# Zero products ahead of the first weights, factors spread by TensorE, both token halves in turn in a hand-set order, and the last products by column halves

## The chip, the cores and the metric

The kernel runs on one core of one Trainium2 chip. The metric is the device time of one execution in microseconds; three executions of the kernel before were timed, and one execution was profiled instruction by instruction.

## The reference

Two transformer blocks are applied to 256 tokens of 1024 features, all in fp32: nine sublayers, each with a norm before and after and a residual. Only the first and the last of them are touched by the change. The first sublayer begins with

```python
def rms_norm(x, g):
    y = x * lax.rsqrt(jnp.mean(x * x, axis=-1, keepdims=True) + EPS)
    return y * g

h = rms_norm(x, pre_mix_g)
z = h @ w_in                       # 1024 -> 2560 columns
za, zb, zc = z[..., :512], z[..., 512:2048], z[..., 2048:]
# za: gelu, then a gated spatial unit; zb: attention of 8 heads;
# zc: gated by a sigmoid, then a causal convolution of 31 taps
```

and the last one ends with `h + 0.5 * rms_norm(f, g)`, where `f` is the feed-forward's down projection of 2816 hidden features.

## The kernel before

**Tiling.** The tokens lie in two halves of 128 on the partitions. All weights come from memory as one stream of 452 pieces of 128 x 1024 fp32 in the order of their use (`w_dma`, line 113, issued by SyncE into four `raw` slots). Each piece is split into a hi part (`w_hi`, ScalarE, line 126) and a lo part (`w_lo`, VectorE, line 135), which go to one of eleven `whl` slots; a `raw` slot is free after the lo part. Operands are split in the same way (`hilo`, lines 187 and 188), and each product is three TensorE products: hi by hi, hi by lo, lo by hi (`mm3`, lines 182 to 184, or `piece_pass`, line 376).

**Order.** The program is traced once; a scheduler then sets each engine's order by its own estimate of the times, taking the instructions by the order of the trace where several are ready. Weight splits count as traced 300 instructions later. On the chip every engine takes its instructions in that fixed order.

**Memory.** Slots of SBUF (`sml`, `big`) and the eight banks of PSUM are handed out in turn: the one that was given back first is taken first.

**Start.** `run` loads the first half of `x`, the identity, the first norm's gains (host-made copies for all 128 partitions, two tiles of 128 x 512), three weight pieces, the second half of `x`, further pieces. ScalarE squares both rows of 512 columns (`squares`, line 258), GpSimd makes r in two instructions (`rsqrt2`, lines 217 and 220), VectorE makes h (`pre_vec`, line 246), TensorE transposes it (`feat4`, line 330), and `hilo` makes the feature-major parts. The second half's norm is a generator (`rest`) that `xstage` steps on beneath the first half's products.

**First products.** `xstage` runs eight k-tiles of 1024 columns for the first half of the tokens (48 products of 512 columns), keeping the eight pieces; then, in the mixer, `mid` makes the first gated tile of the convolution's input (`glu(0)`, 48 products of 256 columns) and loads the memory; then the same eight pieces serve the second half. `each` does Gelu, a layer norm and the values of a half. `glu(1)` comes after that; then `bg` holds the convolution's taps, which `pump` traces by three.

**End.** `boundary` ends each sublayer: the last seven k-tiles of the first half by column halves, its norm (`chain`), the last seven of the second half k-tile by k-tile, the two column halves within each. For the last sublayer the generator's tail (lines 277 to 295) is the end of the program.

## Time and profile before

| | us |
|---|---|
| three runs | 1443.32, 1440.42, 1439.56 |
| median | 1440.42 |
| profiled execution: span from first to last instruction | 1443.3 |
| profiled execution: its own time, the first of the three runs | 1443.32 |

The span and the time of that execution agree, so nothing lies outside the span. The rows below are from this one execution; it is the slowest of the three, 0.2% above the median. Times in rows are counted from the span's start. TensorE is PE (PEld its weight loads), VectorE is DVE, ScalarE is ACT, GpSimd is POOL, SyncE is SP.

### The profile page before, as it was taken

What the parts mean: (1) busy time and instruction counts of PE and PEld (TensorE: products, weight loads), DVE (VectorE), ACT (ScalarE), POOL (GpSimd) and SP (SyncE); (2) the same over time, 40 slices, a digit from 0 to 9 for tenths busy, and PEclk for the clock granted to TensorE, in tenths of its full rate; (3) what the DMA queues carried; (4) which work ended last, traced back from release to release, by engine and by line L of the source; (5) the groups of instructions that cost most, each with busy time, mean ns of one, the idle gap of its engine ahead of it and who ended that gap; (6) DMA issues with size and microseconds to landing.
All of it is one profiled execution on the core that took longest, in us unless ns stands there. A gap on an engine that the chain in (4) does not pass through costs nothing.

```text
span 1443.3 us, 22986 instructions
## 1 busy us (share of the span) xinstructions
PE 1406.3 (97%) x9052; PEld 1271.7 (88%) x9052; DVE 924.2 (64%) x1283; ACT 749.7 (52%) x1226; POOL 141.7 (10%) x160
## 2 busy tenths in 40 slices
PE   7999999999999999999899999999999998999998
PEld 5887998999989999889779999899998887899997
DVE  5998857655566555679776555665556798665552
ACT  6775645544455445466564444554445665554441
POOL 1132001000010000136410000100001132100000
PEclk9999999999999999999999999999999999999999
DMA  8735644655547555453256555475555543365540
GB/s 272 267 106 203 206 146 166 221 191 191 186 154 241 185 197 202 161 175 118 103 198 211 190 187 182 153 239 189 196 193 176 203 153 124 132 219 189 179 159 30
DMA packets 77276, 259.49 MB, mean 180 GB/s; under 512 B 8816, under 2 KB 10224, under 8 KB 77168
## 3 DMA queue, kind: packets, MB, share of 16 engines
q1 hardware_dynamic: 77168, 258.02, 52.1%
q8 instruction: 71, 1.16, 0.3%
q14 instruction: 37, 0.30, 0.1%
HBM read 256.94 MB, written 1.05 MB: 179 GB/s over the span
## 4 chain that ended last, share of the span: by engine, by line
PE 54%; issue 32%; DVE 6%; POOL 3%; ACT 2%; DMA 2%; SPq 0%; POOLq 0%; DVEq 0%; ACTq 0%
PE bank L182 15%; PE bank L183 15%; PE bank L184 15%; PE bank L376 6%; DVE whl L135 2%; DMA raw<-in_w 2%; PE bank L330 1%; ACT whl L126 1%; POOL st L217 1%; PE bank L660 1%; POOL st L220 1%; PE bank L903 1%; DVE sml L607 1%; PE bank L617 0%; DVE sml L651 0%
## 5 line engine op out<-in xcount | busy, mean ns | idle before, releaser
L135 DVE TENSOR_TENSOR whl<-raw,whl 128x1024 fp32r<-128x1024 f32 x448 | 550.8, 1236 | 284.1 <-ACT whl L126 281.3
L126 ACT ACTIVATE whl<-raw 128x1024 fp32r<-128x1024 f32 x452 | 474.1, 1056 | 327.3 <-PE bank L184 164.1
L182 PE MATMUL bank<-big,whl 128*128 128x256 f32 x1824 | 519.9, 285 | 0.0
L184 PE MATMUL bank<-big,whl 128*128 128x256 f32 x1824 | 517.5, 284 | 0.2 <-DVE whl L135 0.2
L183 PE MATMUL bank<-big,whl 128*128 128x256 f32 x1824 | 517.7, 284 | 0.0
L182 PEld LDWEIGHTS bank<-big,whl 128*128 128x128 f32 x1824 | 351.1, 192 | 4.4 <-issue 0.2
L183 PEld LDWEIGHTS bank<-big,whl 128*128 128x128 f32 x1824 | 351.0, 192 | 3.2
L184 PEld LDWEIGHTS bank<-big,whl 128*128 128x128 f32 x1824 | 350.9, 192 | 0.4 <-DVE whl L135 0.4
L182 PE MATMUL bank<-whl,big 128*128 128x512 f32 x640 | 253.1, 396 | 0.0
L183 PE MATMUL bank<-whl,big 128*128 128x512 f32 x640 | 250.7, 392 | 0.0
L184 PE MATMUL bank<-whl,big 128*128 128x512 f32 x640 | 249.3, 391 | 0.0
L376 PE MATMUL bank<-whl,big 128*128 128x512 f32 x768 | 181.1, 394 | 2.5 <-ACT big L187 2.5
L376 PEld LDWEIGHTS bank<-whl,big 128*128 128x128 f32 x768 | 144.6, 190 | 33.1 <-ACT big L187 3.2
L184 PEld LDWEIGHTS bank<-whl,big 128*128 128x128 f32 x640 | 120.4, 188 | 25.9
L182 PEld LDWEIGHTS bank<-whl,big 128*128 128x128 f32 x640 | 120.9, 189 | 22.3
L183 PEld LDWEIGHTS bank<-whl,big 128*128 128x128 f32 x640 | 120.9, 189 | 21.0
L217 POOL TENSOR_SCALAR st<-st 128x1 f32<-128x1 f32 x38 | 18.4, 485 | 917.9 <-ACT sml L277 839.5
L520 ACT ACTIVATE sml<-bank 128x256 f32<-128x256 f32 x72 | 27.7, 384 | 129.4 <-PE bank L184 129.4
L521 DVE TENSOR_TENSOR sml<-sml,bank 128x256 f32<-128x256 f32 x72 | 30.4, 422 | 71.3 <-ACT sml L520 71.3
L187 ACT ACTIVATE big<-bank 128x512 fp32r<-128x512 f32 (+2 forms) x81 | 43.9, 565 | 36.8 <-PE bank L330 30.9
L188 DVE TENSOR_TENSOR big<-bank,big 128x512 fp32r<-128x512 f32 (+2 forms) x81 | 51.1, 652 | 15.4 <-ACT big L187 15.0
L280 DVE SCALAR_TENSOR_TENSOR sml<-bank,sml 128x512 f32<-128x512 f32 x36 | 24.1, 687 | 51.1 <-ACT sml L277 51.0
(161 smaller groups left out, 1018.8 us busy)
## 6 DMA issues: line engine op xcount, KB each, us to landing
raw<-in_w SPq DMA_DIRECT2D x452, 512.0 KB, 3.3
sml<-in_gains SPq DMA_DIRECT2D x38, 256.0 KB, 3.7
sml<-in_na_bias SPq DMA_DIRECT2D x16, 256.0 KB, 3.1
sml<-in_alibi SPq DMA_DIRECT2D x8, 192.0 KB, 4.1
x<-in_x SPq DMA_DIRECT2D x4, 256.0 KB, 5.5
big<-in_mem SPq DMA_DIRECT2D x1, 1024.0 KB, 5.8
out_x<-x SPq DMA_DIRECT2D x4, 256.0 KB, 2.1
sml<-in_gate_ln SPq DMA_DIRECT2D x1, 256.0 KB, 6.1
```

Of the source, the lines that this page charges most:

```text
L126: self.nc.scalar.activation(out=t[:, 0], in_=raw, func=AF.Copy)
L135: eng.tensor_sub(out=t[:, 1], in0=raw, in1=t[:, 0].bitcast(F32))
L182: mm(out, lhsT=ah, rhs=bh, start=first, stop=False)
L183: mm(out, lhsT=ah, rhs=bl, start=False, stop=False)
L184: mm(out, lhsT=al, rhs=bh, start=False, stop=last)
L187: self.nc.scalar.activation(out=hi, in_=src, func=AF.Copy)
L188: self.nc.vector.tensor_sub(out=lo, in0=src, in1=hi.bitcast(F32))
L217: self.nc.gpsimd.tensor_scalar(out=t, in0=a, scalar1=b, scalar2=EPS, op0=ALU.add, op1=ALU.add)
L280: nc.vector.scalar_tensor_tensor(out=t, in0=acc[j], scalar=factor, in1=self.post_g[j], op0=ALU.mult, op1=ALU.mult)
L376: self.nc.tensor.matmul(acc[j], lhsT=x, rhs=p[:, part, c], start=first, stop=last)
L520: nc.scalar.activation(out=t[:, 0], in_=outs[0], func=AF.Silu)
L521: nc.vector.tensor_tensor(out=t[:, 0], in0=t[:, 0], in1=outs[1], op=ALU.mult)
```

## The change

- `run`: the gain tiles of 128 x 512 are no longer loaded at the start; two rows of 1 x 512 (`grow`) are. A tile of zeros (`warm`, 128 x 512) and a row of ones are filled by VectorE. One weight piece instead of three is asked for before the second half of `x`. The first half's norm is not made in `run`.
- The mixer calls `xstage_both` instead of `xstage`. In it the order of TensorE, ScalarE and VectorE is the written one up to the second k-tile: 10 products of zeros into a bank that is never read; two products of the ones by the gain rows, which put the factors on all partitions in two banks; 8 products of zeros; the first half's norm and transposes, each followed by 2 products of zeros; the weight splits between; the second half's norm; both halves' products with the first two k-tiles. From the third k-tile on the two halves take turns with each piece, in the scheduler's order. `glu(0)` and the memory's load come after all of it.
- `squares2`: one row of 512 columns by ScalarE, the other by VectorE.
- `last_half`: the last sublayer's second half takes all seven k-tiles for the first 512 columns, then for the others; the first columns' square, its EPS and its product with the gains are traced between. GpSimd adds the two mean squares and takes the power; the two stores go out on SyncE's and on ScalarE's queue.

Comments and docstrings are gone too; `hilo` and `feat4` return an instruction that nobody uses.

```diff
+    def squares2(self, half):
+        ss = self.st(2)
+        junk = [self.S.get([128, 512]) for _ in range(2)]
+        x = [self.x[:, half, 512 * j : 512 * j + 512] for j in range(2)]
+        self.nc.scalar.activation(
+            out=junk[0], in_=x[0], func=AF.Square, scale=1.0 / 32, accum_out=ss[:, 0:1]
+        )
+        self.nc.vector.tensor_tensor_reduce(
+            out=junk[1], in0=x[1], in1=x[1], scale=1.0 / 1024, scalar=0.0,
+            op0=ALU.mult, op1=ALU.add, accum_out=ss[:, 1:2],
+        )
...
+    def xstage_both(self, ft, specs, each, early=None):
+        nc = self.nc
+        junk = self.B.get([128, 512])
+        gb = [self.B.get([128, 512]) for _ in range(2)]
+        acc = [[self.B.get([128, 512]) for _ in range(2)]]
+        ps = {}
+        def idle(n):
+            for _ in range(n):
+                nc.tensor.matmul(junk, lhsT=self.warm[:, 0:128], rhs=self.warm, start=True, stop=True)
+        def split():
+            self.w_hi()
+            self.w_lo()
+        def products(half, k):
+            if k not in ps:
+                ps[k] = self.W(specs[k])
+            xh, xl = self.kt(ft, k, half)
+            self.piece_pass(acc[half], xh, ps[k], 0, k == 0, False)
+            self.piece_pass(acc[half], xh, ps[k], 1, False, False)
+            self.piece_pass(acc[half], xl, ps[k], 0, False, k == KT - 1)
+        engines = {mybir.EngineType.PE, mybir.EngineType.Activation, mybir.EngineType.DVE}
+        with self.tc.manual_schedule(engines=engines):
+            idle(10)
+            for j in range(2):
+                nc.tensor.matmul(gb[j], lhsT=self.ones, rhs=self.grow[j], start=True, stop=True)
+            idle(8)
+            h0 = self.pre_vec(0, self.squares2(0), gb)
+            split()
+            for j in range(2):
+                self.feat4(0, h0[j], ft[j])
+                idle(2)
+            split()
+            ss = self.squares2(1)
+            h1 = self.pre_vec(1, ss, gb)
+            split()
+            products(0, 0)
+            products(0, 1)
+            for j in range(2):
+                self.feat4(1, h1[j], ft[j])
+            split()
+            self.S.put(*h0, *h1, *self.start_tiles)
+            self.B.put(junk, *gb)
+            acc.append([self.B.get([128, 512]) for _ in range(2)])
+            for k in range(2):
+                products(1, k)
+                self.done(ps.pop(k))
+        for k in range(2, KT):
+            for half in range(2):
+                products(half, k)
+                if k == KT - 1:
+                    each(half, acc[half])
+            self.done(ps.pop(k))
+            if k == 4 and early is not None:
+                early()
...
+        if self.pre_g is None:
+            self.last_half(acc[1], lag1, ch, factor)
+            return dst
...
+    def last_half(self, acc, lag, ch, factor):
...
+        for j in range(2):
+            c = slice(512 * j, 512 * j + 512)
+            for n, (first, lhs, get, _) in enumerate(lag):
+                xh, xl = lhs(1)
+                p = get()
+                self.mm3(acc[j], xh, xl, p[:, 0, c], p[:, 1, c], first, n == len(lag) - 1)
+                if not j and n in (1, 3, 5):
+                    next(ch, None)
...
+            nc.scalar.activation(
+                out=junk, in_=acc[j], func=AF.Square, scale=1.0 / 32, accum_out=ss[:, j : j + 1]
+            )
+            if not j:
+                nc.vector.tensor_scalar(
+                    out=ss[:, 2:3], in0=ss[:, 0:1], scalar1=EPS, scalar2=None, op0=ALU.add
+                )
+            nc.vector.scalar_tensor_tensor(
+                out=yg[j], in0=acc[j], scalar=factor, in1=self.post_g[j], op0=ALU.mult, op1=ALU.mult
+            )
...
+        nc.gpsimd.tensor_tensor(out=r, in0=ss[:, 1:2], in1=ss[:, 2:3], op=ALU.add)
+        nc.gpsimd.tensor_tensor(out=r, in0=r, in1=self.mhalf[:, :1], op=ALU.pow)
+        for j in range(2):
...
+            nc.vector.scalar_tensor_tensor(out=xs, in0=yg[j], scalar=r, in1=xs, op0=ALU.mult, op1=ALU.add)
+            q = nc.scalar if j else nc.sync
+            q.dma_start(out=self.out[128:256, c], in_=xs)
...
-        self.xstage(ft, [(("w_in", 0, k, 0, 512), ("w_in", 0, k, 1536, 512)) for k in range(KT)], each, mid, early)
+        self.xstage_both(ft, [(("w_in", 0, k, 0, 512), ("w_in", 0, k, 1536, 512)) for k in range(KT)], each, early)
+        mid()
...
+        grow = [self.S.get([1, 512]) for _ in range(2)]
+        ones = self.S.get([1, 128])
+        nc.vector.memset(ones, 1.0)
+        warm = self.S.get([128, 512], F32R)
+        nc.vector.memset(warm.bitcast(F32), 0.0)
         load_x(0)
+        for j in range(2):
+            row = GAIN_ROWS.index(GAINS[self.phases[0]][0])
+            nc.sync.dma_start(out=grow[j], in_=self.aps["gains"][row, 0:1, 512 * j : 512 * j + 512])
         nc.sync.dma_start(out=self.ident, in_=self.aps["ident"])
-        g = self.load_gain(GAINS[self.phases[0]][0])
-        self.w_dma(3)
+        self.w_dma(1)
         load_x(1)
         self.w_dma()
...
-        h0 = self.pre_vec(0, self.squares(0), g)
-        self.pump()
-        self.to_feat(0, h0, ft)
-        def rest():
...
```

## Rows read from the trace of the kernel before

**Rows 1.** The page, its first line and its part 1 (busy us, share of the span, instructions), the whole execution.

```profile
span 1443.3 us, 22986 instructions
...
PE 1406.3 (97%) x9052; PEld 1271.7 (88%) x9052; DVE 924.2 (64%) x1283; ACT 749.7 (52%) x1226; POOL 141.7 (10%) x160
```

**Rows 2.** The list of waits of TensorE over the whole execution: instruction and line <- what ended the wait: us in total, times, longest us.

```profile
PE bank L330 <- DVE sml L246: 10.9, 4, 7.9
...
PE bank L617 <- DVE sml L607: 6.7, 6, 2.2
...
PE bank L376 <- ACT big L187: 2.5, 1, 2.5
```

**Rows 3.** The timeline of the first 35 us: start us, duration us, engine, line, operation, out<-in, count [idle before <- what ended it]. SPq is SyncE issuing DMAs.

```profile
0.72 0.86 SPq L1504 DMA_DIRECT2D x<-in_x  x2
...
0.80 0.07 DVE L100 MEMSET mhalf<- 128x16 f32 x1 [0.80 <-PEq L1633]
...
5.64 0.57 POOL L220 TENSOR_TENSOR st<-st,mhalf 128x1 f32<-128x1 f32 x1
...
7.06 1.44 DVE L246 SCALAR_TENSOR_TENSOR sml<-x,st,sml 128x512 f32<-128x512 f32 x2 [6.19 <-DMA sml<-in_gains]
...
7.86 1.97 PE L330 MATMUL bank<-ident,sml 128*128 128x128 f32 x8 [7.86 <-DVE sml L246]
...
9.46 1.06 ACT L126 ACTIVATE whl<-raw 128x1024 fp32r<-128x1024 f32 x1 [4.31 <-DMA raw<-in_w]
...
10.73 1.06 ACT L126 ACTIVATE whl<-raw 128x1024 fp32r<-128x1024 f32 x1 [0.21 <-DMA raw<-in_w]
...
11.69 1.07 ACT L187 ACTIVATE big<-bank 128x512 fp32r<-128x512 f32 x2
...
12.32 6.94 PE L376 MATMUL bank<-whl,big 128*128 128x512 f32 x20 [2.50 <-ACT big L187]
```

**Rows 4.** The instructions of tile `x` issued from 1.1 us to 1.6 us (the loads of the first two rows of 512 columns): us from issue to landing.

```profile
DMA to landing us min/median/max: 2.9/3.0/3.1
```

**Rows 5.** Timelines of TensorE in windows of 0.2 us (a row merges the products that the window holds; its first number is the start of the first of them).

```profile
13.34 1.05 PE L376 MATMUL bank<-whl,big 128*128 128x512 f32 x2
...
13.77 1.05 PE L376 MATMUL bank<-whl,big 128*128 128x512 f32 x2
...
17.04 0.62 PE L376 MATMUL bank<-whl,big 128*128 128x512 f32 x2
...
17.26 0.63 PE L376 MATMUL bank<-whl,big 128*128 128x512 f32 x2
```

**Rows 6.** Four stretches (us from the span's start): length, then busy us and instructions of TensorE, its weight loads, VectorE, ScalarE, GpSimd; the granted clock; the share of the DMA engines; GB/s.

```profile
12.32:43.55 31.23, 31.03 (x152) 26.25 (x153) 24.91 (x32) 20.16 (x26) 2.99 (x5) 1.00 0.81 272
...
43.55:58.10 14.55, 14.55 (x121) 14.34 (x119) 13.64 (x27) 12.89 (x18) 0.98 (x2) 1.00 0.83 298
...
58.10:61.40 3.30, 2.09 (x11) 1.50 (x11) 3.08 (x9) 1.88 (x2) 0.00 (x0) 0.97 0.85 305
...
61.40:64.80 3.40, 3.40 (x18) 3.40 (x18) 3.22 (x10) 2.88 (x7) 0.00 (x0) 0.52 0.24 87
```

**Rows 7.** The timeline of the end, columns as in rows 3.

```profile
1436.77 0.39 PE L184 MATMUL bank<-whl,big 128*128 128x512 f32 x1
...
1437.20 0.60 ACT L277 ACTIVATE sml<-bank 128x512 f32<-128x512 f32 x1
...
1437.98 0.30 POOL L217 TENSOR_SCALAR st<-st 128x1 f32<-128x1 f32 x1 [8.57 <-DVE sml L280]
...
1438.37 0.56 POOL L220 TENSOR_TENSOR st<-st,mhalf 128x1 f32<-128x1 f32 x1
...
1439.74 0.99 SPq L295 DMA_DIRECT2D out_x<-x  x2
```

**Rows 8.** VectorE's groups of instructions by line and shape in the first 44 us: out<-in, shapes, count | busy us, mean ns | idle before.

```profile
L135 DVE TENSOR_TENSOR whl<-raw,whl 128x1024 fp32r<-128x1024 f32 x15 | 18.1, 1221 | 5.2 <-ACT whl L126 5.2
...
L1225 DVE SCALAR_TENSOR_TENSOR sml<-sml,dw,sml 128x256 f32<-128x256 f32 x6 | 2.9, 481 | 0.1
...
L246 DVE SCALAR_TENSOR_TENSOR sml<-x,st,sml 128x512 f32<-128x512 f32 x4 | 2.9, 750 | 7.0 <-DMA sml<-in_gains 6.2 <-POOL st L220 0.9
...
L188 DVE TENSOR_TENSOR big<-bank,big 128x512 fp32r<-128x512 f32 x4 | 2.7, 686 | 0.5 <-ACT big L187 0.5
```

**Rows 9.** The same view of VectorE over the whole execution: the smaller sums (here a sum and a running minimum) that one instruction makes with its product.

```profile
L1339 DVE CUSTOM_DVE_ANT_0 sml<-bank,sml 128x256 f32<-128x256 f32 x8 | 3.4, 419 | 0.0
```

**Rows 10.** ScalarE's groups in the first 62 us: the loads of function tables ahead of Gelu and Sigmoid.

```profile
L1174 ACT ACT_TABLE_LOAD x2 | 2.6, 1283 | 0.0
...
L1245 ACT ACT_TABLE_LOAD x2 | 2.6, 1283 | 0.0
```

**Rows 11.** The timeline of TensorE in the first mixer: plain fp32 products of 64 columns.

```profile
91.04 0.78 PE L1370 MATMUL bank<-sml,sml 128*128 128x64 f32 x6
```

**Rows 12.** The timeline of 54 to 67 us, around the first scores.

```profile
54.64 1.99 ACT L126 ACTIVATE whl<-raw 128x1024 fp32r<-128x1024 f32 x2
...
58.26 0.49 DVE L1225 SCALAR_TENSOR_TENSOR sml<-sml,dw,sml 128x256 f32<-128x256 f32 x1
...
59.25 0.38 PE L659 MATMUL bank<-sml,sml 128*128 128x256 f32 x1 [1.14 <-DVE sml L647]
```

**Rows 13.** The timeline of TensorE, a later wait of the same mixer.

```profile
128.63 0.33 PE L342 MATMUL bank<-ident,big 128*128 128x128 f32 x1 [1.69 <-DVE big L1381]
```

More of the change, by code (lines that the diff above doesn't have):

```diff
@@ L186, in hilo @@
     def hilo(self, hi, lo, src):
-        self.nc.scalar.activation(out=hi, in_=src, func=AF.Copy)
+        made = self.nc.scalar.activation(out=hi, in_=src, func=AF.Copy)
         self.nc.vector.tensor_sub(out=lo, in0=src, in1=hi.bitcast(F32))
+        return made
     def table(self, func):
@@ L262, in squares @@
         self.S.put(junk)
+        return ss
+    def squares2(self, half):
[9 more added lines that the diff above has]
+        )
+        self.S.put(*junk)
         return ss
@@ L332, in feat4 @@
         sl = slice(128 * half, 128 * half + 128)
-        self.hilo(dst[:, 0, k0 : k0 + n, sl], dst[:, 1, k0 : k0 + n, sl], s)
+        made = self.hilo(dst[:, 0, k0 : k0 + n, sl], dst[:, 1, k0 : k0 + n, sl], s)
         self.B.put(b)
+        return made
     def feat_both(self, src, dst, n, k0):
@@ L439, in boundary @@
         return dst
+    def last_half(self, acc, lag, ch, factor):
+        nc = self.nc
+        ss, r = self.st(4), self.st()
+        yg = [self.S.get([128, 512]) for _ in range(2)]
+        for j in range(2):
[6 more added lines that the diff above has]
+                    next(ch, None)
+            junk = self.S.get([128, 512])
+            nc.scalar.activation(
[8 more added lines that the diff above has]
+            )
+            self.S.put(junk)
+        for _, _, get, after in lag:
+            self.WHL.put(get())
+            if after is not None:
+                after()
+        nc.gpsimd.tensor_tensor(out=r, in0=ss[:, 1:2], in1=ss[:, 2:3], op=ALU.add)
+        nc.gpsimd.tensor_tensor(out=r, in0=r, in1=self.mhalf[:, :1], op=ALU.pow)
+        for j in range(2):
+            c = slice(512 * j, 512 * j + 512)
+            xs = self.x[:, 1, c]
+            nc.vector.scalar_tensor_tensor(out=xs, in0=yg[j], scalar=r, in1=xs, op0=ALU.mult, op1=ALU.add)
+            q = nc.scalar if j else nc.sync
+            q.dma_start(out=self.out[128:256, c], in_=xs)
+        self.S.put(*yg, *self.post_g)
+        self.B.put(*acc)
     def later(self, spec):
@@ L1506, in load_x @@
                 )
+        grow = [self.S.get([1, 512]) for _ in range(2)]
[3 more added lines that the diff above has]
+        nc.vector.memset(warm.bitcast(F32), 0.0)
         load_x(0)
+        for j in range(2):
+            row = GAIN_ROWS.index(GAINS[self.phases[0]][0])
+            nc.sync.dma_start(out=grow[j], in_=self.aps["gains"][row, 0:1, 512 * j : 512 * j + 512])
         nc.sync.dma_start(out=self.ident, in_=self.aps["ident"])
-        g = self.load_gain(GAINS[self.phases[0]][0])
-        self.w_dma(3)
+        self.w_dma(1)
         load_x(1)
         self.w_dma()
+        self.warm, self.start_tiles = warm, (warm, ones, *grow)
+        self.ones, self.grow = ones, grow
         ft = self.new_feat()
-        h0 = self.pre_vec(0, self.squares(0), g)
-        self.pump()
-        self.to_feat(0, h0, ft)
-        def rest():
-            h1 = self.pre_vec(1, self.squares(1), g)
-            self.S.put(*g)
-            yield
-            for j in range(2):
-                self.feat4(1, h1[j], ft[j])
-                self.S.put(h1[j])
-                yield
-        self.pend = rest()
         self.mt = None
```

## The prediction, made before the change was run

> **What bounds the kernel now.** I read the page first, then who waited for whom on TensorE, then the timeline of the first 65 us and of the last 10, because the diff touches only these two stretches. The reader should see on the page that TensorE is busy 97% of a 1443.3 us span, 37 us short of it [rows 1]. The list of waits says where those 37 us are: 7.9 us before the first transposes, 2.5 us before the first weight product, and else short ones far from the diff, such as six that make 6.7 us [rows 2]; the last 6 us are the end of the last norm. So in the middle TensorE sets the time, and the change can win only what TensorE loses at the two ends.
>
> At the start the chain is: x lands, ScalarE squares it, GpSimd makes r (ready at 6.2), VectorE waits for the gain rows until 7.06, TensorE transposes, then waits for ScalarE, which splits two weight pieces before it comes to the transposes' copy at 11.69; the first weight product starts at 12.32 [rows 3]. These products start 0.43 us apart at 13.8 and 0.22 to 0.23 apart from 17.04 on [rows 5]: 512 columns in 0.43 us is the 1.2 GHz level, in 0.23 the 2.4 GHz one (the view prints a granted clock of 1.00 there, from before its first record). From 12.32 to 43.55, when the second gated tile's products begin, TensorE is busy 31.03 of 31.23 us [rows 6]. 43.55 is the mark against which I sum: by then both kernels must have done 96 wide products, the second half's 8 transposes and the 48 narrow products of the first gated tile.
>
> At the end, the last product starts at 1436.77, and squares, GpSimd's two steps, the residual and the store follow one behind the other to 1443.3 [rows 7].
>
> **The change, part by part, start.** *Zeros and factors.* TensorE can begin when VectorE has filled the zero tile. A 128x16 fill takes 0.07 us [rows 3], any 128x512 instruction of two inputs 0.75 at most [rows 8]; I take 0.5, so 1.5 us. Ten products at 0.43 end at 5.8. Then come the two products that spread the factors, plain fp32, 512 columns. The nearest rows: 0.23 us for 512 columns of the other kind [rows 5], or 8 times that of fp32 products of 64 columns, six of which take 0.78, 0.10 to 0.13 each: 0.8 to 1.0 [rows 11], both at 2.4 GHz, twice that at 1.2. They are of the second kind, so I take 0.88 each. The clock rose 4.7 us after the stream of products began [rows 3, 5]; here that would be 6.2, so the first is done near 6.8, the second at 7.6, and eight more zero products end at 9.4 (8.1 with the cheap price).
>
> *The norm of the first half.* The squares are shared out: the second half row lands at 1.15 + 3.1 = 4.3 [rows 3, 4], and VectorE's squared sum of 512 columns costs about 0.7 (0.42 for 256 [rows 9]). r is ready at 6.05 where it was 6.2. The 6.2 us wait for the gain rows goes, but what is late next is the spread factor itself: h is made from 6.9 to 8.5, where it was 7.06 to 8.50. The factor change alone is worth nothing. It does take 0.5 MB out of the queue: the first weight piece has 1.1 MB up to and with it instead of 1.6 MB, so it should land near 7.7 instead of 9.45. The second piece has the same 2.06 MB as before and lands at 10.7 as before [rows 3].
>
> *First products.* Transposes 9.4 to 9.95, copy 10.0 to 10.6 (0.60), two zero products, the other transposes, copy to 11.6; the first weight product starts at 11.25 instead of 12.32, and at the high level: 1.1 us and 2.3 us won (11 products at 0.43 instead of 0.23 [rows 5]).
>
> *What the hand-set order queues.* VectorE and ScalarE now work in written order. Behind the copy stands the second piece's hi part (1.06, to 12.65), behind that VectorE's lo part (1.22 [rows 8], to 13.9), only then the second half's squared sum (14.6), GpSimd (0.95 for its two steps [rows 7], 15.7) and h (twice 0.75, to 17.2), the third piece's lo part (18.4), the lo part of the second half's first tile (0.69 [rows 8], 19.1). TensorE has only 12 products for this time. It does eight to 13.1, waits for the lo part until 13.95, ends at 14.9, waits for h until 16.5, transposes until 17.7 and does one product. The next one writes the bank that the first transposes of the second half used (banks are handed out in turn: 0 to 4 go to the zeros, the factors and the first half's sums, the four sets of transposes get 5, 6, 7 and 5, so the second half's sums get 6 and 7), so it waits for VectorE's reading of it, 19.15. Before, the same norm ended beneath 48 products and cost TensorE nothing. From there 11 + 72 products at 0.227 and 48 of 256 columns at 0.12 (121 in 14.55 us [rows 6]) take TensorE to 43.75. Against 43.55: +0.2. Without a wait 11.25 and 28.45 of work would make 39.7; the waits of 0.85, 1.6 and 1.4 and some small ones give it back.
>
> The other bound: the cheap factor price, so that only the second piece's landing (10.7) holds the chain: all of it 0.85 earlier, 42.9, which is -0.65. I take the middle, -0.2.
>
> *Elsewhere in the mixer.* Both halves' Gelu now stand together, before the gated products: of the two loads at each of these two lines one may go (1.28 us each on ScalarE [rows 10]). ScalarE is not what TensorE waits for there, so I count 0; the cover is TensorE's 14.55 busy us of 14.55 [rows 6]. The taps of the convolution that VectorE did before 44 us (six in 2.9 us [rows 8]) must come later, in exchange for weight pieces split earlier: 0, if VectorE has room (a rival below). The small loads and the memory's load go out some us later on SyncE's queue behind the weight pieces; they are used from 60 us on, or in the layer norm at 38.
>
> **End.** The same 42 products by column halves. The first columns' square leaves the tail, but it was no part of it: the second square began at 1437.20, after the last product at 1436.77, and the one before it was over by then [rows 7]. The multiply by gains ran beside GpSimd. GpSimd now adds two tensors instead of adding scalars (0.30): 0.30 to 0.56, the price of its power on the same shape [rows 7]; I take 0.4, +0.1. Two stores on two queues instead of one: the second waited for its half of the residual, not for the first store, so 0. A store from ScalarE's queue is not in the trace; SyncE's loads and stores took 0.43 and 0.50 each [rows 3, 7], so 0 with 0.1 either way.
>
> **Sum.** -0.2 + 0.1 = -0.1. The profiled execution's span, 1443.3, is that of the slowest of the three runs, 1443.32; against the median of 1440.42 the sum gives 1440.3 us. What a measurement of this kernel can tell from no change is about 0.3%, 4.3 us: from 1436.1 to 1444.7.
>
> **Rivals.**
> *The waits I worked out don't come, and one behind goes too (faster).* If the second half's norm comes in time (the order of squares and lo parts takes less than I count), TensorE reaches the mark at 40.1 (39.7 and 0.4 of small waits): 3.4 less. After that the first scores wait 1.14 us for VectorE, which is behind a tap and for ScalarE, which is behind two hi parts; the clock is then 0.52 for 3.4 us, worth 1.7 [rows 6, 12]. The work around them is scheduled anew and ScalarE has fewer table loads; without them it is 2.8 less. Together -6.2: 1434.2. For it: those waits rest on nine durations in a row, and a queue that runs an instruction sooner shortens all. Against: each of them is a measured row, and none is counted with a gap.
>
> *The clock falls inside the stage.* From 14.9 to 19.15 TensorE would have about 1.2 us of work. Such a stretch cost the clock at 58: 1.14 idle with light work behind it, then 0.52; 1.69 idle at 128.6 did not [rows 6, 12, 13]. A fall costs 1.7: 1442.0. The Trainium skill, "TensorE: Matmul & The Clock Gate", Part 4, says that transposes don't count as work for the clock as products do; by that the stretch is nearly empty, and this case would be the likely one. The trace here agrees only loosely: the eight transposes at 7.86 [rows 3] did not keep the products at 12.32 from the low level, but 2.5 us of waiting lay between.
>
> *VectorE gets behind (slower).* From 43.55 to 61.4 VectorE is busy 16.7 of 17.85 us [rows 6]. If these taps and the gated product move behind 44 us (2.9 + 0.4, say 3.4 us, with no weight pieces done ahead for it), scores and probabilities wait behind them in its queue: 3.4 and a fall of the clock behind it, 1.7: +5.1, 1445.5. It decides from the point where the pieces split by 44 us are no more than the 15 of before [rows 8].
>
> *The zeros do not raise the clock.* Then 1.2 GHz lasts until the real products have run: factors done at 9.3, zeros at 12.7, first product near 16.1, second half's h at 20.7, the mark near 48: +4.5, 1444.9. Against: nothing but that no row here shows products of zeros.
>
> **Chances.** As summed 0.42; clock falls in the stage 0.20; faster rival 0.22; VectorE behind 0.11; zeros without effect 0.05. The first two are within 0.3%: same 0.62, faster 0.22, slower 0.16. The likeliest is 1440.3. The range runs from just below the faster rival, 1433, to the zeros' case, 1445; a third of the faster case and the VectorE case are left out (0.18).
>
> **What would show it.** Right: the first wide product with weights near 11.3 and 0.23 us apart; waits of TensorE for VectorE's h near 15 to 17 and for a bank near 18; the first products of the second gated tile within a us of 43.5; the last product to the end of span still 6.5 us. Wrong: no such waits, or a mark near 40; a longer gap before the first scores; a granted clock of 0.5 between 18 and 23.

## The result: 12.5 us slower, and the profile after

The changed kernel takes 1454.35 us (median of 4 runs, 1453.95 to 1456.41); the kernel before, run beside it, takes 1441.87 (4 runs, the three above and one of 1443.36). The ratio is 1.0087, 95% interval 1.0069 to 1.0106. The prediction was 1440.3, no change, and none of its rivals reached beyond 1445.5. One run of e2, of 2773.8 us, is left out of its figures below.

One thing about the numbers first. In the runs whose span is on record, those of the kernel before too, the time lies 1.73 to 1.86 us above the span (2.07 to 2.16 in e8). I had taken the span of 1443.3 [rows 1] for the whole time of that execution; by this its time was about 1445.1, and it is none of the three timed runs. It lies 3 us above the median of the kernel before, so the 8.9 us between the two profiles' spans understate the difference of the medians by some 3 us.

The page of the changed kernel, first line and part 1:

```profile
span 1452.2 us, 23043 instructions
...
PE 1420.9 (98%) x9078; PEld 1282.8 (88%) x9078; DVE 922.8 (64%) x1290; ACT 747.0 (51%) x1220; POOL 142.6 (10%) x160
```

TensorE is busy 14.6 us longer than before [rows 1], with 26 more products recorded (the zeros and the factors), and it is short of the span by 31 us instead of 37. That does not mean that it waits less where it matters: 9.8 of the 14.6 us lie ahead of the first weight product, where it stood idle before. From that product to the end (columns as in [rows 6]), first in the kernel before, then in the changed one:

```profile
12.32:1443.33 1431.01, 1404.38 (x9044) 1270.10 (x9044) 921.00 (x1279) 744.35 (x1218) 140.34 (x152) 0.99 0.52 179
```

```profile
13.41:1452.16 1438.75, 1409.07 (x9045) 1274.63 (x9043) 918.08 (x1281) 743.11 (x1215) 141.34 (x152) 0.99 0.54 177
```

There the changed kernel is 7.7 us longer: busy 4.7 longer, for the same products (9044 and 9045 records), and idle 3.0 longer. A product at the lower clock counts as busy for longer (products of zeros start 0.22 us apart at 8.6 and 0.42 apart at 9.6).

The timeline of the start, changed kernel (start us, duration us, engine, line, operation, out<-in, count, [idle before <- what ended it]):

```profile
1.60 4.61 PE L433 MATMUL bank<-sml 128*128 128x512 f32 x10 [1.60 <-DVE sml L1633]
...
6.14 1.98 PE L451 MATMUL bank<-sml,sml 1*128 1x512 f32 x4
...
7.37 1.54 DVE L247 SCALAR_TENSOR_TENSOR sml<-x,st,bank 128x512 f32<-128x512 f32 x2 [2.43 <-issue]
...
8.05 2.58 PE L433 MATMUL bank<-sml 128*128 128x512 f32 x8
...
10.43 1.06 PE L346 MATMUL bank<-ident,sml 128*128 128x128 f32 x4
...
11.67 0.38 SPq L1121 DMA_DIRECT2D big<-in_mem  x1
...
13.41 2.06 PE L393 MATMUL bank<-whl,big 128*128 128x512 f32 x8
...
16.36 1.33 POOL L1392 TENSOR_TENSOR sml<-sml,sml 128x512 f32<-128x512 f32 x1 [3.07 <-DMA sml<-in_tri]
...
17.79 0.30 POOL L218 TENSOR_SCALAR st<-st 128x1 f32<-128x1 f32 x1
...
19.59 1.89 PE L346 MATMUL bank<-ident,sml 128*128 128x128 f32 x8 [1.93 <-DVE sml L247]
```

The zeros run from 1.60, the factor products from 6.14 to 8.05, and the first weight product starts at 13.41 (12.32 before [rows 3]). SyncE sends for the memory at 11.67. GpSimd multiplies the mask at 16.36, ahead of the second half's r at 17.79, and TensorE waits 1.93 us for that half.

Stretches of the changed kernel, columns as in [rows 6]; the granted clock is the third number from the end:

```profile
6.09:9.50 3.41, 3.41 (x11) 1.90 (x11) 2.09 (x3) 1.06 (x1) 0.09 (x1) 1.00 1.01 334
9.50:12.91 3.41, 3.41 (x14) 2.73 (x12) 1.23 (x2) 0.60 (x1) 0.00 (x0) 0.50 1.03 386
...
46.64:64.10 17.46, 14.56 (x122) 14.35 (x120) 16.04 (x28) 13.10 (x18) 0.57 (x1) 1.00 0.77 251
64.10:70.90 6.80, 6.55 (x25) 5.65 (x26) 5.30 (x15) 3.94 (x8) 0.00 (x0) 0.50 0.19 69
91.40:94.80 3.40, 3.40 (x17) 3.40 (x18) 2.44 (x8) 0.91 (x2) 0.00 (x0) 0.50 0.02 5
```

The clock is up at 6.09 and down again from 9.5 to 12.9. It falls once more behind the wait of 1.93, at 19.7 for 3.4 us. From 64.1 it is down for 6.8 us, where before it was down for 3.4 [rows 6], and at 91.4 for 3.4, where before it was up.

The mark, the start of the second gated tile, is at 46.64 instead of 43.55. From there to the first scores (the first products of queries and keys with each other, in the attention) TensorE has the same 14.55 us of work as before [rows 6]. What stands ahead of these scores, changed kernel:

```profile
58.90 1.04 ACT L126 ACTIVATE whl<-raw 128x1024 fp32r<-128x1024 f32 x1
60.34 1.06 ACT L126 ACTIVATE whl<-raw 128x1024 fp32r<-128x1024 f32 x1 [0.40 <-DMA raw<-in_w]
61.31 0.36 ACT L762 ACTIVATE sml<-bank 64x256 fp32r<-64x256 f32 x1
...
59.02 2.46 DVE L1345 SCALAR_TENSOR_TENSOR sml<-sml,dw,sml 128x256 f32<-128x256 f32 x6
61.40 1.22 DVE L135 TENSOR_TENSOR whl<-raw,whl 128x1024 fp32r<-128x1024 f32 x1
...
64.35 0.58 PE L779 MATMUL bank<-sml,sml 128*128 128x256 f32 x1 [3.15 <-DVE sml L767]
```

The products of the first queries and keys end near 58.3 (the mark and two gated-size tiles of 5.8). ScalarE makes their hi and lo parts only at 61.31, behind two weight pieces, one of which it waits for; VectorE does six taps and a split meanwhile. TensorE waits 3.15 us, where it waited 1.14 [rows 12].

So the 8.9 us between the profiles arise thus: 3.1 up to the mark, 2.0 from it to the first scores, 2.9 from there to the first norm's squares (at 136.27 before, 144.29 after), and 0.9 in the other 1300 us.

The end, changed kernel:

```profile
1445.68 0.39 PE L184 MATMUL bank<-whl,big 128*128 128x512 f32 x1
...
1446.87 0.19 POOL L550 TENSOR_TENSOR st<-st 128x1 f32<-128x1 f32 x1 [8.55 <-ACT sml L535]
...
1449.18 0.38 ACTq L557 DMA_DIRECT2D out_x<-x  x1
```

From the last product to the end of the span it is 6.5 us, as before (6.6).

### The profile page after: what moved, and what is told of

The parts are those of the page before. It is cut to its first block, busy times and chain, and to the rows that moved or that the text cites. A ratio compares the mean times of both kernels' runs of the same rounds, so it can differ in the third digit from the quotient of the medians.

```text
span 1452.2 us, 23043 instructions
## 1 busy us (share of the span) xinstructions
PE 1420.9 (98%) x9078; PEld 1282.8 (88%) x9078; DVE 922.8 (64%) x1290; ACT 747.0 (51%) x1220; POOL 142.6 (10%) x160
## 4 chain that ended last, share of the span: by engine, by line
PE 55%; issue 31%; DVE 6%; POOL 3%; DMA 2%; ACT 2%; POOLq 0%; DVEq 0%; ACTq 0%; SPq 0%
PE bank L182 15%; PE bank L183 15%; PE bank L184 15%; PE bank L393 5%; DMA raw<-in_w 2%; DVE whl L135 2%; ACT whl L126 1%; PE bank L346 1%; PE bank L780 1%; POOL st L221 1%; POOL st L218 1%; PE bank L779 1%; DVE sml L727 1%; PE bank L737 0%; PE bank L1023 0%
```

## The experiments

"Before" is the kernel before, run beside each; times are medians. Letters name theories of what loses the time, as their texts use them: A, the start and the mixer behind it; B, the second store queue costs time outside the span; C, the gated products come late; D, chance in the scheduler's order; E, the mask multiply ahead of r; S, the order of both halves in turn; L, loads issued early; V, VectorE's sum of work; O, the order of work on VectorE.

**The end.**

```
e1: before, with the changed end (last_half)
e2: changed, with both last stores on nc.sync
```

> The kernel before with the last sublayer's end by column halves alone (its two stores on SyncE's and ScalarE's queues). The start is that of before. Theory A (the whole loss comes from the start and the mixer behind it): the end inside the span is shorter by 0.1, so the time is that of before, 1441.9 within 1. Theory B (a store on a second queue costs about 1.75 us outside the span, since the changed kernel's times are 1.75 above its spans and those of before equal theirs): 1.6 more, 1443.5, with the span unchanged.

> The changed kernel with both last stores on SyncE's queue. Theory B: the time falls by 1.75 to about 1452.6, and time and span agree again. Theory A: 1454.3, with time and span still 1.75 apart.

e1: 1442.38 against 1442.61, ratio 1.000 (0.9987 to 1.0014). e2: 1452.07, ratio 1.0074 (1.0046 to 1.0101). The end is worth nothing that shows within 2 us, and B is dead: time and span differ by the same 1.8 us with one queue and with two. Both are of further use below: in their profiles every engine of e1 has the order of the kernel before up to the last norm, and every engine of e2 that of the changed kernel, so they are second executions of the same order.

**The gated tile early; GpSimd in written order too.**

```
e3: changed, with mid() and its pieces behind the fifth k-tile
e4: changed, with   engines = {PE, Activation, DVE, + Pool}
```

> The changed kernel with the first gated tile's products (and their two weight pieces, and the memory's load) after the fifth k-tile instead of after the eighth. Theory C (VectorE is behind at the first scores, because the convolution's taps can only start after the gated tile): taps run before 44 us again, the wait before the first scores falls from 3.15 to 1 or less, the fall of the clock there from 6.8 us to 3.4 or none: 4 to 5 less, 1449.5. Theory D (the loss after 46 us is chance of the scheduler's order, whatever VectorE does): no less than 2 us gained. The loss of 3.1 us up to the mark stays in both.

> The changed kernel with GpSimd among the engines whose order is the written one. In the changed kernel GpSimd multiplies the spatial weights by their mask (1.33 us, after its load) ahead of the second half's r. Theory E (that multiply makes the second half's h late): r comes 1.2 us earlier, h at 17.5 instead of 18.78, the wait of TensorE before the second half's transposes falls from 1.93 to about 0.7, the mark (end of the first gated tile) from 46.6 to 45.4, the time to 1453.1. The rival: TensorE waits for the lo part of the second piece and the bank anyway, and the mark moves by less than 0.5.

e3: 1455.46, ratio 1.0096 (1.0075 to 1.0117); nothing won, and the wait for the first scores grew to 4.6 us. That leaves C open rather than dead: one tap ran before 44 us (six in the kernel before), and 12 stood ahead of the first scores, as many as in the changed kernel. e4: 1451.26, ratio 1.0069 (1.0043 to 1.0095). The edit missed its aim: the mask multiply still ran ahead of r, since the written order holds inside its block alone. So e4 is, engine by engine and from start to end, a third execution of the changed order. Its profile is of its shortest run, 1445.9, while the three others took 1449.8 to 1452.9: the same program, 4 to 7 us apart, and one execution only 3.3 us over before. In the profiled one the clock doesn't fall between 25.3 and 649.9 us, and the wait for the first scores is 0.82 us; ScalarE and TensorE there:

```profile
58.61 1.06 ACT L126 ACTIVATE whl<-raw 128x1024 fp32r<-128x1024 f32 x1 [0.26 <-DMA raw<-in_w]
59.58 0.36 ACT L763 ACTIVATE sml<-bank 64x256 fp32r<-64x256 f32 x1
...
62.76 0.38 PE L780 MATMUL bank<-sml,sml 128*128 128x256 f32 x1 [0.82 <-DVE sml L768]
```

The mark is 0.7 us later than in the changed kernel's profile, but the piece ahead of the parts is split at 58.61 instead of 60.34, the parts begin at 59.58 instead of 61.31, and the first scores at 62.76 instead of 64.35. In e2 the three times are 61.63, 62.59 and 65.81, the wait 3.44. One order, three executions: the scores come 3.0 to 3.2 us after the parts begin, and the parts come right behind that piece.

**The parts alone.**

```
e5:  before + a tile of zeros; 18 products of it ahead of the first transposes, 6 behind each four
e6:  changed start, but then   self.xstage(ft, ..., each, mid, early)   as before
e12: before's start and end, with xstage_both (no zeros, gains as tiles)
```

> The kernel before with one thing added: VectorE fills a tile of zeros, TensorE makes 18 products of it before the first transposes and 6 after each of the two groups of four. What the warm clock alone is worth: before, the 11 products from 12.32 to 16.9 ran 0.43 us apart instead of 0.23, which is 2.3 us. If the clock that the zeros raise holds through the start, the mark (start of the second gated tile's products, 43.55 before) comes at 41.2 and the time is 2 to 2.5 us under before's, provided that nothing behind takes it back. If it falls between the zeros and the first products, as it did in the changed kernel at 9.5 us, the mark stays within 1 us of 43.55 and the time within 1 us. If VectorE alone sets the mixer's time (theory V below), the mark is earlier but the first norm's end (136.3 before) is not.

> The changed kernel with its start (zeros, spread factors, shared squares, written order up to the first half's transposes) but with the old order behind it: first half, first gated tile, second half, with the second half's norm beneath the first half's products. Theory S (the order of both halves in turn loses the time: the second half's norm in the open, and the first gated tile late, so that the convolution's taps come late): first product near 13.4 as in the changed kernel, no wait for the second half's h, mark between 42 and 44, the wait for the first scores back to about 1 us, time within 3 us of before's. If instead the start itself does the harm (the factors' products and the fall of the clock behind them), the mark stays near 46 and the time 8 to 12 us over before's.

> The kernel before (its start without zeros, its squares on ScalarE, its gains as tiles, its end) with only the stage changed: both halves in turn in the written order, the gated products behind. Theory S (the order loses it): 7 to 10 us over before's time; the mark 2 to 4 us late, for the second half's norm in the open; the wait for the first scores 3 us or more instead of 1.14, since both halves' Gelu, gate norms and gated products fall between the mark and the scores, and a longer fall of the clock behind it. If the loss needs the new start together with the order, this kernel is within 3 us of before's.

| kernel | time | before | ratio (95%) |
|---|---|---|---|
| e5 | 1443.58 | 1441.91 | 1.0009 (0.9992 to 1.0025) |
| e6 | 1446.27 | 1441.91 | 1.0025 (1.0011 to 1.0039) |
| e12 | 1450.34 | 1443.93 | 1.0045 (1.0027 to 1.0062) |

The start loses 4.4 us and the order 6.4, each give or take 2, in all 10.8 of the 12.5. e12's mark is at 42.17, earlier than in before's profile and level with e1's 42.04: the second half's norm in the open costs next to nothing there, against what S expected. What follows the mark does it, here the timeline of e12's first scores, and then its stretches:

```profile
60.73 0.58 PE L764 MATMUL bank<-sml,sml 128*128 128x256 f32 x1 [4.00 <-DVE sml L752]
```

```profile
42.17:60.50 18.33, 14.56 (x122) 14.35 (x120) 17.28 (x31) 12.47 (x19) 2.95 (x3) 1.00 0.83 302
60.50:67.30 6.80, 6.58 (x25) 5.68 (x26) 5.79 (x16) 2.54 (x3) 0.00 (x0) 0.50 0.72 244
```

VectorE is busy 17.28 of 18.33 us, TensorE waits 4.00, and the clock is down for 6.8 us (and again from 81.0). e5 is the contrast; its stretches:

```profile
11.25:55.96 44.71, 43.75 (x273) 38.95 (x273) 39.57 (x60) 34.23 (x44) 3.98 (x7) 1.00 0.86 303
55.96:100.00 44.04, 43.34 (x284) 37.06 (x285) 41.66 (x97) 35.37 (x86) 15.92 (x13) 1.00 0.44 143
```

Its first product comes at 11.25, its mark at 41.19, and the clock stays up from 4.7 to 643 us. Yet its median is no better than before's. In this profile 2.2 of the 4.8 us that it is ahead at 150 us are lost by the last product, and other runs of before are as fast as it.

**What stands ahead of the first scores.**

```
e7:  changed, gains loaded as tiles of 128 rows, idle(18) for idle(10), two factor products, idle(8)
e8:  changed, SIDE_TAPS = 10 (one more tile slot)
e9:  changed, one column of lng, wst, tri and the memory written from h1 before they are loaded
e10: changed, the taps released behind qk_parts(0), which writes a column of their sum (one more slot)
e11: e7 and e10 together
```

> The changed kernel with the norm's factors loaded as two tiles of 128 rows, as before, instead of one row that TensorE spreads; 18 products of zeros follow one another. Everything behind is as changed. Theory: the two factor products (0.9 us each, light work for TensorE) are what the clock fell behind, at 9.5 us in the changed kernel, and what put the first product at 13.41. In the kernel with zeros alone, without them, the clock rose at 4.7, did not fall again, and the first product came at 11.25. Then here: no fall at 8 to 10, first product 11.2 to 11.7, mark about 44.5 instead of 46.6, time 2 to 4 us lower than the changed kernel's. If the fall belongs to the pauses between zeros, transposes and products, it comes here too, and the time stays within 1 us.

> The changed kernel with ten of the convolution's taps on ScalarE and GpSimd instead of six (and one more tile slot, without which they don't fit). It takes 8 instructions of 0.48 us from VectorE, 3.9 us, between the mark and the end of the mixer, and gives ScalarE 8 of 0.5. Theory V (VectorE, which idles only 1.5 of 17.7 us before the first scores, sets the mixer's time): the time falls by 3 to 6 us, the wait of 3.15 us for the first scores shrinks. If TensorE with its falls of the clock sets it (theory S or L), the mark does not move and the time falls by less than 2 us.

> The changed kernel with the small loads of the mixer and the load of the memory held back: each of four tiles gets one column written by VectorE from the second half's h, so that its load cannot start before about 20 us. In the changed kernel SyncE issued them at 5.7 to 11.7 us, ahead of weight pieces, 1.8 MB that take 4.6 us at 0.4 MB per us; before, it issued them at 23 to 37. Theory L (the early loads delay the weight pieces, VectorE and ScalarE idle for them and have less done when the scores begin; and the mask multiply stands ahead of the second half's r on GpSimd): the second half's transposes 1 us earlier, the mark at 43.5 to 44.7, the wait for the first scores at most 2, the time 4 to 8 us lower. Theories S and V: only the mask multiply's 1.0 us, time 0 to 1.5 us lower.

> The changed kernel with VectorE's taps of the convolution held back until the first two heads' parts of queries and keys are made (VectorE writes one column of the taps' sum from them; one more tile slot). Theory O (order on VectorE: taps and splits that the scheduler placed ahead stand before the parts that the first scores wait for; the wait and the fall of the clock behind it cost about 2 + 3.4 us): the mark unchanged, the wait for the first scores under 1 us instead of 3.15, no fall of 6.83 us behind it, the time 4 to 6 us lower than the changed kernel's. Theory V (VectorE's sum of work sets the time): the wait goes, but the taps come later and the first norm's end stays within 2 us of 144.3.

> Both edits in one: factors as tiles, taps held back. If both causes hold and are independent, the gains add up: 6 to 10 us under the changed kernel, which is within 4 us of before's on either side; what is left then is the second half's norm, which TensorE waits for in the open. If only one holds, the time is that of the better of the two.

e7: 1454.48, ratio 1.0081 (1.0053 to 1.0109). The first product comes at 10.19, the clock doesn't fall at 9.5, the mark is at 41.56, all as expected; and none of it is left in the time. The list of waits of e7's TensorE, 40 to 100 us:

```profile
PE bank L776 <- DVE sml L767: 4.3, 1, 4.3
```

An earlier mark only waits longer; from 58.5, within that wait, the clock was down for 10.2 us.

e8: 1455.3, ratio 1.0084 (1.0057 to 1.0111). VectorE's taps from 40 to 146 us, columns as in [rows 8], first in the changed kernel, then in e8:

```profile
L1345 DVE SCALAR_TENSOR_TENSOR sml<-sml,dw,sml 128x256 f32<-128x256 f32 x48 | 23.1, 527 | 0.2
```

```profile
L1345 DVE SCALAR_TENSOR_TENSOR sml<-sml,dw,sml 128x256 f32<-128x256 f32 x40 | 23.1, 620 | 0.1
```

Eight taps fewer, and the same 23.1 us: so V was not tested by this run, since VectorE's taps took as long as before.

e9: 1451.08, ratio 1.0061 (1.0038 to 1.0084), between what L and its rivals expected. The mask multiply went to 28.4, the second half's transposes waited 0.87 instead of 1.93; but the wait for the first scores was 4.0 (the clock rose late there, at 14.4, and the mark came at 47.27). So E holds for about 1 us of wait there, and nothing of it is left at the scores. e10: 1457.33, ratio 1.0095 (1.0067 to 1.0124): O falls as I put it; without a tap ahead a wait of 2.65 us was left, VectorE standing idle 2.2 us for a piece that ScalarE had not split. e11: 1447.59, ratio 1.0042 (1.0025 to 1.0059): neither edit wins alone, together 6.5 us.

**The landing places.** ScalarE stood behind a piece that had not landed, so the next runs give the pieces a fifth place.

```
e13: changed,             Slots(big, "raw", 5)
e14: e5,                  Slots(big, "raw", 5)
e15: changed, five until the end of the mixer (a place given back there is not reused)
e16: e7, the same      e17: before, the same      e18: e5, the same
```

> The changed kernel with five places for weight pieces to land instead of four. Before the first scores ScalarE, which works in written order, waits 2.3 us for pieces that have not landed, with the parts of the first queries and keys behind them (they begin 3 us after their products end). If the landing places are what makes it wait, one more takes most of that away: the wait for the first scores at most 1.5 us, no fall of 6.83 us behind it, the time 3 to 6 us lower. If VectorE's sum of work before the scores (theory V, 18.5 us of work in 17.7) sets them, the wait stays near 3 us and the time within 1.5 us.

> The kernel with zeros alone (old order, gains as tiles) with five places for weight pieces to land. A try at one that beats both: the zeros gave the mark 2.4 us earlier in the trace but no time that could be measured. If waits for pieces take the gain back later, one more place keeps it: 1436 to 1440. If not, the time stays at 1441 to 1444.

> The changed kernel with five landing places during the mixer only; the fifth is taken out at its end, so that later phases run as before. With five places throughout, the first norm's squares came at 135.6 instead of 144.3, but the stretch from 723 to 1243 us was 5.7 longer and the time only 2 lower. If the landing places are the cause of the wait for the first scores: squares at 135 to 138, later stretches as in the changed kernel (1301 us from there to the last product), time 6 to 9 us under the changed kernel's, 3 to 6 over before's. If the gain at 135.6 was one lucky profile, the time is at 1452 to 1455.

> The same with the factors loaded as tiles instead of spread by TensorE. A try at one that beats both: first product near 10.3 (it was 10.20 with tiles and four places), mark near 41.5, wait for the first scores 1 us, no fall of the clock over 3.4 us behind it, squares at 132 to 134 where before has 136.3: 1439 to 1443, level with before's or a little under it.

> The control for the fifth place: the kernel before with five landing places during the mixer only. In the changed kernel the fifth place gave back 8 to 10 us. If it is a cure for what the change brought (ScalarE standing behind pieces that have not landed, before the first scores), it does little here, where that wait is 1.14 us: within 3 us of before's time. If it is worth the same to any order, this kernel is 6 us or more faster than before, and the changed order is not what loses the time.

> The kernel before with zeros alone and five places in the mixer only: the last try at one that beats both. The zeros put the mark at 41.2 and the first norm's squares at 131.7 in one profile, and five places throughout lost it in a later phase. If both hold: 1437 to 1440. If the order around the scores is made worse by the fifth place, as with five throughout (squares at 135.7, a fall of 10.2 us at 73): 1442 to 1446.

| kernel | time | before | ratio (95%) |
|---|---|---|---|
| e13 | 1452.58 | 1443.93 | 1.0068 (1.0044 to 1.0091) |
| e14 | 1454.64 | 1443.93 | 1.0079 (1.0062 to 1.0096) |
| e15 | 1445.85 | 1443.47 | 1.0018 (1.0002 to 1.0034) |
| e16 | 1451.47 | 1443.47 | 1.0063 (1.0043 to 1.0083) |
| e17 | 1448.34 | 1442.18 | 1.0046 (1.0029 to 1.0063) |
| e18 | 1445.53 | 1442.18 | 1.0024 (1.0010 to 1.0037) |

e15 gives back 10 of the 12.5 us (ratio 1.0018 for 1.0087) with the changed start and the changed order both in place. Its ScalarE and TensorE at the first scores:

```profile
58.63 0.38 ACT L767 ACTIVATE sml<-bank 64x256 fp32r<-64x256 f32 x1 [0.20 <-PE bank L189]
...
63.24 0.38 PE L784 MATMUL bank<-sml,sml 128*128 128x256 f32 x1 [1.77 <-DVE sml L772]
```

ScalarE now waits for the product and not for a piece; the wait is 1.77, the clock falls for 3.4 us behind it and not at 91. What is left of the wait lies on VectorE, which does seven taps and a split (57.9 to 61.9) before its share. The two profiles, the changed kernel's and e15's, differ by 5.1 us only, and by as much at 160 us already; the rest of the 10 is between executions that were not profiled. In e13 and e14, with five places throughout, a later phase (from about 723 to 1243 us) is 5.4 to 5.7 us longer than without, which hid the gain of e13; e14 had lost 5.0 against e5 just behind its first scores. e16 and e18, meant to beat both kernels, missed: behind their first scores the clock was down for 10.24 us each.

But e17, the control, is 6.2 us slower than before, so the fifth place is no cure in itself. Its first scores come at 56.69 without a wait. Then come these, in the timeline of e17's TensorE, and behind them a stretch:

```profile
71.84 0.38 PE L664 MATMUL bank<-sml,sml 128*128 128x256 f32 x1 [0.81 <-DVE sml L652]
72.43 0.33 PE L1362 MATMUL bank<-ident,sml 128*128 128x128 f32 x1 [0.21 <-ACT sml L1352]
73.40 0.43 PE L335 MATMUL bank<-ident,sml 128*128 128x128 f32 x1 [0.64 <-POOL sml L1028]
```

```profile
73.50:83.70 10.20, 10.20 (x37) 8.24 (x38) 7.14 (x17) 6.60 (x18) 5.35 (x4) 0.50 0.12 37
```

Three short waits within 2.4 us, 1.66 us in all, and the clock is down for 10.2 us behind them. The Trainium skill, "TensorE: Matmul & The Clock Gate", Part 1, under "A second HAM failure mode", says that frequent short pauses between groups of products make the clock swing; these rows agree, as far as one fall can.

What all profiles say together. Us; e1 has before's order up to there, e2 and e4 the changed one; the stretch runs from the first score's product to the 540th TensorE record behind it:

```
kernel    mark   first score  waited   stretch  at lower clock  stretch less half of that
before    43.55     59.25      1.14     96.60        3.41             94.89
e1        42.04     57.23      0.64     96.54        3.41             94.83
e5        41.19     55.96      0.22     95.07        0                95.07
e12       42.17     60.73      4.00    100.77       13.45             94.05
changed   46.64     64.35      3.15    100.05        9.97             95.07
e2        47.81     65.81      3.44    101.34       13.07             94.81
e4        47.38     62.76      0.82     95.72        0                95.72
e7        41.56     60.43      4.32    102.19       15.11             94.63
e15       46.91     63.24      1.77     95.90        3.41             94.19
e17       42.30     56.69      0       100.11       10.24             94.99
```

In all 20 kernels the last column is 94.0 to 96.3, while the stretch itself goes from 95.1 to 103.1. So in this stretch neither VectorE's sum of work nor the pieces set the time; TensorE does, and what differs, but for some 2 us, is for how long its clock is down. V falls with that. S is right on the wait for the scores and the fall behind it, wrong on the mark, and a little high on the amount (7 to 10 expected, 6.4 measured).

## Why the prediction was wrong

**Right.** The zeros start at 1.60 (1.5), raise the clock at 6.09 (6.2), the factor products take 1.9 together (0.88 each), the first piece lands at 7.54 (7.7), the wait for the second piece's lo part is 0.53 (0.85). The end is -0.1 instead of +0.1, and worth nothing, as e1 measured. GpSimd's add, 0.4 in my sum, took 0.19.

**The first product: 13.41, not 11.25.** The step that failed is "at the high level": I took the clock that the zeros raise to stay up. It fell at 9.5, behind the two factor products, which read one row, and made zeros, transposes and copies 1.3 to 1.7 us late; the rest of the 2.2 is the factors, done at 8.1 instead of 7.6. In e13, with the same start and no fall, the first product came at 12.07. In the six profiles with zeros and without factor products (e5, e7, e11, e14, e16, e18) the clock stays up from its rise (4.5 to 7.3) past the mark; in the ten with them it either fell at 8.2 to 9.6 (four), or rose only at 13.9 to 14.4 (five), and stayed up once (e13). My own rival, the clock falling in the light stretch ahead of the second half, came true at 19.7; the fall at 9.5, among the zeros, I had in no rival.

**The second half's h: transposes at 19.59, not 16.5.** Two of these us are the late first product; 1.2 are GpSimd's mask multiply ahead of r. I wrote that the small loads and the memory's "go out some us later". They went out at 5.7 to 11.7 instead of 22.95 to 36.92 (SyncE is not among the engines in written order), and the mask's landing released the multiply. The wait of 1.4 for a bank did not come. I had counted 12 products ahead of these transposes; 14 ran there, so the scheduler had moved products of the third k-tile up, and TensorE went on behind the transposes without a wait.

**Behind the mark: +5 us where I put 0.** This is the other step that failed, the cover: "ScalarE is not what TensorE waits for there, so I count 0", with TensorE's 14.55 busy us as what hides it, and "0, if VectorE has room". Both halves' Gelu, gate norms and gated products now fall into this stretch together with the splits, and the parts of the first queries and keys stand behind them on ScalarE and VectorE. TensorE's busy time covers only what is done when it ends, and its next product needed those parts. I had something like this as a rival: 3.4 us of taps and 1.7 of clock, decided by whether more than 15 pieces are split by 44 us. 14 were split by then (15 by the mark), so by its own test it held, and I gave it 0.11. Its cause was only half right, since the parts stood behind a piece on ScalarE and not behind VectorE's taps alone, and its price had the wrong shape: the wait grew by 2.0, and the clock behind it was down 6.6 us longer, 3.3 us of time. A wait was not to be counted by its length; 1.14 before was followed by 3.4 us of lower clock, 3.15 by 6.8 and a second fall at 91.

**The sum of it.** e12, where the start is as before: mark -1.4, wait +2.9, clock (13.45 - 3.41) / 2 = +5.0, together +6.5. The two profiles differ by 5.7 up to the stretch's end (the last column is 0.8 lower) and by 5.9 in all; that the medians differ by 6.4 is near to the sum by luck. The changed kernel: mark +3.1, +2.0 to the scores, (9.97 - 3.41) / 2 = +3.3, together 8.4 of the 8.9 between its profile and that of before. Most of the rest of the 12.5 is that profile of before, 3 us above its median. e1's, with the same start, is 2.0 shorter, and has all of that by the first scores. Against it the changed kernel's profile is 10.9 longer: 4.6 up to the mark, 2.5 more to the scores, 3.5 in the stretch behind, 0.3 after it.

**Open.** That the wait for the first scores and the falls behind it hold over half of the loss, and the late mark the rest, is shown by the table: against e1's profile 6.0 and 4.6 us. That the wait hangs on the piece ahead of the parts is shown by e4, where the order is the changed one, that piece is split 1.7 us sooner, and wait and falls are all but gone; why the pieces came sooner in that execution is not known. Whether e15 cures the same thing, or merely has another plan, which the fifth place makes the scheduler write, is not settled: in e17 the same place made a worse one. Nor is it known why the clock fell for 3.4 us in one run and for 6.8 or 10.2 in another. No version beat the kernel before; e1 and e5 are level with it.

## What to carry to other kernels

Before a stage is reordered, follow the next product that needs another engine's result, and list what the new order puts ahead of that result on each in-order engine; TensorE's own busy time is no cover for it. Where light products stand close to short waits, price the wait by the clock that it may cost, here from nothing (e4) to three times the wait itself (e17), and look at several executions before calling a profile typical: two of the kernel before are 1.5 us apart at the mark, three of the changed order 3 us apart at the first scores. An earlier mark is worth nothing until the next wait has been looked at: e7 reached it 2 us before the old kernel's profile and lost 12.

## What the runs showed of the hardware

- Products of zeros raise the clock as others do: up some 3 to 6 us after they begin in the six profiles without factor products. Two products that read one row, 1.9 us long together in the changed kernel, were followed by a fall or a late rise in nine of ten.
- Three waits of 0.81, 0.21 and 0.64 us near light products were followed by 10.2 us at the lower clock, 5.1 us of time (e17); one of 1.77 by 3.4 us of it (e15); one of 0.82 by none (e4).
- Taking eight of 48 taps from VectorE saved it nothing: the other 40 went from 527 to 620 ns, while GpSimd's adds of 128x512 rose from 7.5 to 15.0 us in all (e8). Of the 40, the 14 that overlap such an add take 886 ns on average, the 26 others 476. The Trainium skill, "Advanced Engine Details and Errata", "GPSIMD Details", says that GpSimd shares a read and a write interface with VectorE and conflicts with its instructions of two SBUF inputs; a tap is one, and the trace agrees.
- Time and span of one execution differ by 1.73 to 1.86 us here, by 2.07 to 2.16 in e8.
